# Stacking the real and imaginary state parts on 128 partitions for the mixer's output products

## The chip, the cores and the metric

The kernel runs on one core of one Trainium2 chip, as one program. The metric is device time in microseconds (us) of one execution. The five engines have their own in-order instruction streams: TensorE (PE in the profile, with its weight loads as PEld), VectorE (DVE), ScalarE (ACT), GpSimd (POOL) and SyncE (SP), which here only issues DMA transfers.

## The reference

One denoising step of a two-layer network with 1024 features, on 128 context tokens and 1024 latent tokens. Each layer has a token mixer and a SwiGLU channel mixer, each followed by a residual and a LayerNorm, with shifts, scales and gates computed from a condition vector (`ada_mod`). The mixer of layer 0 is a bidirectional S5 state space of 64 groups of 16 features with 64 complex states each:

```
bu   = einsum('blgh,gph->blgp', u, bb)            # complex, two directions
s    = linear recurrence of (ab, bu) over l        # forward, and backward
y    = u * d_skip
for d in 0, 1:
    y += einsum('blgp,ghp->blgh', s_re, c_re[d]) - einsum('blgp,ghp->blgh', s_im, c_im[d])
y    = gelu(y);  v = y @ glu_w + glu_b;  out = val * sigmoid(gate)
```

Layer 1 mixes by window means. Outputs are both token streams and the context's final states.

## The kernel before

All arithmetic is fp32. Most of the span is the two layers' weight products on the 1024 latents, which split each operand into two fp32r parts and use three products (L776 to L778). The change is in the state-space mixer of layer 0, which comes before them.

The sequence is cut into chunks of 8 tokens: 128 chunks for the latents (NCL), 16 for the context (NCC). Two groups form a pair, whose states fill 128 partitions: group x of the pair on partitions 64x to 64x+63. A state tile `Z[d]` of direction d is [128, slots, 64], where the last axis is (re or im, 32 group pairs), so the 128 chunk values of one pair and one part lie 64 floats apart. The recurrence over chunks runs on VectorE (`scan_step`, L438 and L443).

The output of a chunk is a sum of products on TensorE: one of the chunk's own inputs `u` with an in-chunk kernel, and one per direction and part of the states with an output table. Tables are built by `ssm_tables` for 8 groups (kt = 0 to 7), sent to DRAM (L509, L544), and fetched again by `load_mo` as one 1.5 MB tile `mo` (L548), once per kt for the context (`ssm_y_ctx`) and once for the latents (`ssm_y`). Because a group's re and im parts lie on the same 64 partitions, each state product has a height of 64: for the latents L611 issues 8 of them per group pair (2 directions, 2 parts, 2 groups), with the table as the stationary operand and `Z` as the moving one. In the context (L566) `Z` is stationary and the table moves. Results of the latents go through a gelu (L616) and to DRAM (`yd`); they are read back as `yr` (L1095), split into xm and xn (L760, L761), and feed the layer's glu product.

Around this, other work fills TensorE: the context's glu and channel mixing (`ffn`, L780; one 512 KB load `raw` feeds 8 products; a later part takes 256 KB loads `rc`), and the modulation `ada` (L148; one 512 KB load `adaw` feeds 4 products). `x_sample` comes in as `xr` (L381) and is transposed (`px`, L386). A timeline scheduler of the framework orders each engine's instructions when the kernel is built, from its own model of costs; buffer counts of the pools (`raw` 3, `adaw` 2, `mo` 3, `yr` 2) bound how far loads run ahead. All weight loads are issued by SP, in order. The result row of the last ada bank (`arow`, `ar`) lies where the pool of `yr` is opened, so the loads of `yr` start only after it. A fp32 product is two matmul records in the profile.

Of the kernel before, what the change touches and what calls it, by code (L numbers as in the profile page):

```python
# [41 lines left out]
class Kernel:  # L42
# [3 lines left out]
    # ---------------------------------------------------------------- helpers  # L46
# [20 lines left out]
    def cmul(self, eng, pool, o_re, o_im, a, b, shape, tag, nb_im=None, p=None):  # L67
        """o = a * b for complex pairs; with nb_im = -b_im the imaginary part comes out negated."""
        (a_re, a_im), (b_re, b_im) = a, b
        given = p  # L70
        for k in range(2):
            if given is None:
                p = pool.tile(shape, F32, tag=tag + "1", name=tag + "1")
            q = pool.tile(shape, F32, tag=tag + "2", name=tag + "2")
            if k == 0:
                eng.tensor_tensor(p, a_re, b_re, op=OP.mult)
                eng.tensor_tensor(q, a_im, b_im, op=OP.mult)
                eng.tensor_tensor(o_re, p, q, op=OP.subtract)
            else:
                eng.tensor_tensor(p, a_re, b_im if nb_im is None else nb_im, op=OP.mult)  # L80
                eng.tensor_tensor(q, a_im, b_re, op=OP.mult)
                eng.tensor_tensor(o_im, p, q, op=OP.add if nb_im is None else OP.subtract)

    # ------------------------------------------------------------- constants
    def consts(self):
        nc, I = self.nc, self.I
        cp = self.cp
        self.ones = cp.tile([128, 128], F32, name="ones")
        nc.vector.memset(self.ones, 1.0 / D)
        self.eps = cp.tile([128, 1], F32, name="eps")  # L90
        nc.vector.memset(self.eps, LN_EPS / (ALPHA * ALPHA))

        r0 = cp.tile([16, 128], F32, name="r0")
        nc.sync.dma_start(r0[0:8, :], I["c"].rearrange("o (k p) -> (o k) p", p=128))
        nc.sync.dma_start(r0[8:16, :], I["c_ctx"].rearrange("(k p) -> k p", p=128))
        p0 = self.psum("pv0")
        nc.tensor.transpose(p0[:, 0:16], r0, self.ident[:16, :16])
        self.cond = cp.tile([128, 8, 32], F32, name="cond")
        nc.vector.memset(self.cond, 0.0)
        nc.scalar.activation(self.cond[:, :, 0:2].rearrange("p k i -> p i k"),  # L100
                             p0[:, 0:16].rearrange("p (i k) -> p i k", i=2), AF.Silu)
        # mod[l]: [128, vec, cond, kt]; vec = sh1, sc1, g1, sh2, sc2, g2
        self.mod = [cp.tile([128, 6, 2, 8], F32, name=f"mod{l}") for l in range(2)]
# [26 lines left out]
    # --------------------------------------------------------- conditioning  # L130
    def ada_steps(self, l, b, pool=None):
        """Columns 2048*b.. of layer l's modulation, for both conditions, in small steps."""
# [45 lines left out]
    # ------------------------------------------------------------------ SSM  # L178
    def ssm_params(self, pool, tmp, ad):
# [31 lines left out]
        self.h0 = self.sk.tile([128, 2, 2, 32], F32, name="h0")   # dir, re/im, gpair  # L211
# [19 lines left out]
        # powers of the discretized diagonal: [128, re/im, exponent 0..8, (dir, gpair)]  # L231
# [12 lines left out]
        # input coefficient  # L244
# [15 lines left out]
        # scan multipliers per direction: [128, dir, (Rr|Rr|-?), ...]  # L260
        rm = self.sk.tile([128, 2, 2, 2, 32], F32, name="rm")      # dir, term, re/im, gpair
# [7 lines left out]
        # B and C with the states on the partitions: [128, re/im, (dir, gpair), 16]  # L269
# [28 lines left out]
    def ssm_modvec(self, pool, tmp, arow):  # L298
        """(1 + sc1) and sh1 per (token in chunk, channel) partition: [128, cond, (sh, sc), g]."""
# [20 lines left out]
    def ssm_u(self, tmp, kt):  # L320
        """u[(s,h), g, chunk]: the modulated mixer input; also the context's residual."""
# [23 lines left out]
    def ssm_u_ctx(self, tmp):  # L345
# [3 lines left out]
        # partitions are (feature tile, chunk)  # L349
# [25 lines left out]
    def load_x(self):  # L375
        """Feature-major residual of the latents."""
# [13 lines left out]
    def ssm_in(self, tmp, d, kt, tp, nb):  # L390
        """Chunk inputs V of direction d's state recurrence for 8 groups, written into the state slots."""
# [41 lines left out]
    def scan_step(self, *steps):  # L433
        """State slots: dst += A^8 src, for each (direction, src, dst); the steps are independent."""
# [37 lines left out]
    def ssm_dskip(self, pool, tmp):  # L472
        """D on the partitions (group of 8, h'): [128, kt]; selector of h == h'; zeroed B blocks."""
# [12 lines left out]
        # block-diagonal B of group pairs: [128 = (group of 2, state), dir, re/im, pair, (group of 2, h')]  # L486
# [4 lines left out]
    def ssm_tables(self, tmp, kt, si):  # L491
        """Output tables and in-chunk kernels of 8 groups, to DRAM in the layout of the output products."""
# [3 lines left out]
        for d in range(2):  # L496
# [12 lines left out]
            nc.sync.dma_start(mo[:, 1024 + 1024 * d:2048 + 1024 * d], tab.rearrange("p r g h j -> p (r g h j)"))  # L509
# [36 lines left out]
    def load_mo(self, tmp, kt):  # L546
        mo = tmp.tile([128, 3072], F32, tag="mo", name="mo", bufs=3)
        self.nc.sync.dma_start(mo, self.mo[kt])  # L548
        return (mo[:, 0:1024].rearrange("p (g m) -> p g m", g=8),
                mo[:, 1024:3072].rearrange("p (d r g m) -> p d r g m", d=2, r=2, g=4))  # L550

    def ssm_y_ctx(self, tmp, kt):
        """Mixer output (after gelu) of the context for 8 groups, feature-major."""
        nc = self.nc
        m, ot = self.load_mo(tmp, kt)
        pss = [self.psum(f"pyc{x}") for x in range(2)]
        for t in range(5):
            for x in range(2):
                for gp in range(4):
# [4 lines left out]
                    else:  # L564
                        d, r = (t - 1) // 2, (t - 1) % 2
                        nc.tensor.matmul(  # L566
                            o, self.Z[d][64 * x:64 * x + 64, NCL + d:NCL + d + NCC, 32 * r + 4 * kt + gp],
                            ot[64 * x:64 * x + 64, d, r, gp, :], start=False, stop=(t == 4))
# [14 lines left out]
        # the last ones stay on chip: partitions (group pair, chunk); a group's features go to its own columns,  # L583
        # the rest of them stay zero
# [12 lines left out]
    def ssm_y(self, tmp, kt):  # L597
        """Mixer output (after gelu) of the latents for 8 groups, to DRAM feature-major."""
        nc = self.nc
        m, ot = self.load_mo(tmp, kt)  # L600
        y = tmp.tile([128, 8, NCL], F32, tag="yl", name="yl", bufs=2)
        py = [self.psum(f"py{x}") for x in range(2)]
        for gp in range(4):
# [4 lines left out]
            for d in range(2):  # L608
                for r in range(2):
                    for x in range(2):  # L610
                        nc.tensor.matmul(  # L611
                            o[x], ot[64 * x:64 * x + 64, d, r, gp, :],
                            self.Z[d][64 * x:64 * x + 64, d:d + NCL, 32 * r + 4 * kt + gp],
                            start=False, stop=(d == 1 and r == 1))
# [77 lines left out]
    def ctx0a(self):  # L692
        """The context's mixer output projection of layer 0."""
# [5 lines left out]
    def ctx0b(self):  # L699
        """The context's channel mixing of layer 0, in steps."""  # L700
# [5 lines left out]
    def ctx1a(self, tmp):  # L706
        """The context's pool mixer."""
# [8 lines left out]
    def ctx1b(self):  # L716
        """The context's channel mixing of layer 1, in steps."""
# [6 lines left out]
    # -------------------------------------------------------- derived vectors  # L724
    def vecs(self, l, b):
        """Per-feature vectors [128, cond, kt] of the residual gates and of LayerNorm + modulation,
        from the b-th pair of the layer's modulation vectors."""
# [22 lines left out]
    # ----------------------------------------------------------------- GEMMs  # L750
    def split(self, pool, src, shape, tag, bufs):
        """src = H + L exactly, both exact in float32r."""
# [10 lines left out]
    def weight(self, b, src, shape):  # L763
        """A block of weights [128, n, m]: raw for the native path, (H, L) for the split one."""
# [21 lines left out]
    def pair(self, b, w, x, name):  # L786
        """Two GEMM tiles that are combined elementwise; w yields their weights."""
# [71 lines left out]
    # ------------------------------------------------------------- LayerNorm  # L859
# [6 lines left out]
    def ln_stats(self, b):  # L866
        """b.x to zero mean and unit variance over the features, in place."""
# [33 lines left out]
    def ln_apply(self, b, l, s, xm=None):  # L901
        """The affine part, in place; with xm, also the modulated input of the channel mixer."""
# [19 lines left out]
    # ------------------------------------------------------------ pool mixer  # L922
    def box(self, pool, src, n_out, k, tag, axis, out=None):
        """Window sums along a zero-padded axis (length n_out + k): src[.., i : i + k]."""
# [18 lines left out]
    def pool_cols(self, tmp, q, gis=range(4)):  # L943
        """Window sums along the grid's rows of its rows 4q .. 4q + 3, summed up over the rows: row r of P holds
        the sum of the rows 0 .. r."""
# [19 lines left out]
    def pool_z(self, tmp, b, i, gi):  # L965
        """(window mean - input) of 8 rows of the grid for one window, split for the product."""
# [75 lines left out]
    # ---------------------------------------------------------------- output  # L1042
    def store(self, b, out, t0):
        """Feature-major [128, 8, tokens] back to rows of tokens."""
# [12 lines left out]
    # ----------------------------------------------------------------- build  # L1057
# [124 lines left out]
class Rows:  # L1182
    """Weights [128, n, m] in tiles of four rows."""
# [39 lines left out]
```

## Time and profile before

| what | us |
|---|---|
| median of 3 runs | 2500.75 (2499.89 to 2501.96) |
| span of the profiled execution, first to last instruction | 2493.0 |
| what lies around it: median less span | 7.75 |
| PE busy in the span | 2296.9 (92%) |
| context's outputs on PE (L566) | 220.9 to 279.1 |
| latents' outputs on PE (L611), the main run | 388.7 to 484.5 |
| loads and first glu products that follow | 484.5 to 581.8 |

The profiled execution has no time of its own beside its span; the 7.75 us are the difference to the median and are taken as fixed. PE's 92% is an average: the first 580 us hold most of its idle time, where weights are loaded, and from about 580 us on it is nearly always busy. What a change in the mixer is worth is read from the stretch between 300 and 640 us.

### The profile page before, as it was taken

Reading aid. Unit: us, or ns where it says so; the run is one execution under the profiler, and the core shown is the slowest. Engines: PE = TensorE matmul, PEld = TensorE weight load, DVE = VectorE, ACT = ScalarE, POOL = GpSimd, SP = SyncE. Lnnn points to the kernel's source line nnn. Section 1 sums busy time; section 2 is a strip of 40 time slices with the busy share of each in tenths; the row PEclk is TensorE's granted clock in tenths of the full one; section 3 lists DMA queues with packets and bytes.
Section 4 is the critical chain, followed back from the end, with each engine's and each line's share of the span. In section 5 each row is a group of like instructions: output and inputs, shape, how many; then the busy total and the mean of one; then the engine's idle time right before and its main releaser. Section 6 shows DMA issues by size and latency. Waiting matters only on the chain.

```text
span 2493.0 us, 33897 instructions
## 1 busy us (share of the span) xinstructions
PE 2296.9 (92%) x13533; PEld 1880.8 (75%) x13533; DVE 1252.8 (50%) x2429; ACT 895.0 (36%) x1321; POOL 191.2 (8%) x190
## 2 busy tenths in 40 slices
PE   4685779979999999999999999889999999999997
PEld 2453557668888788888888888777788888888996
DVE  7579771024444632455422585778422455422476
ACT  3673211134423422433422353325322443322464
POOL 4760000000001000100000010002000100000000
PEclk8897889999999999999999999999999999999998
DMA  7767888796454333223333224874333223333352
GB/s 219 218 203 286 278 262 262 219 313 178 142 156 129 101 93 100 95 98 96 94 98 97 99 96 137 236 204 142 94 96 97 95 93 95 92 97 96 136 202 103
DMA packets 465246, 370.63 MB, mean 149 GB/s; under 512 B 19792, under 2 KB 414816, under 8 KB 462784
## 3 DMA queue, kind: packets, MB, share of 16 engines
q1 hardware_dynamic: 445296, 349.29, 45.5%
q10 hardware_dynamic: 18448, 14.58, 1.8%
q0 software_dynamic: 1344, 4.59, 0.5%
q8 instruction: 106, 1.74, 0.3%
q14 instruction: 52, 0.43, 0.1%
HBM read 345.36 MB, written 22.94 MB: 148 GB/s over the span
## 4 chain that ended last, share of the span: by engine, by line
PE 79%; DMA 13%; ACT 3%; DVE 2%; SPq 1%; issue 1%; POOL 1%; ACTq 0%; DVEq 0%; POOLq 0%
PE ffn L778 13%; PE ffn L776 13%; PE ffn L777 13%; PE dn L777 6%; PE dn L776 6%; PE dn L778 6%; PE ffn L780 4%; DMA adaw<-ada_w 3%; PE py L611 3%; PE dn L780 2%; DMA raw<-ffn_w_up 2%; PE glu L777 2%; PE glu L778 2%; PE glu L776 2%; DMA raw<-ffn_w_gate 2%; PE ada L148 1%
## 5 line engine op out<-in xcount | busy, mean ns | idle before, releaser
L760 ACT ACTIVATE wh<-raw 128x1024 fp32r<-128x1024 f32 (+1 forms) x326 | 341.6, 1049 | 944.0 <-PE ffn L777 619.6
L761 DVE TENSOR_TENSOR wl<-raw,wh 128x1024 fp32r<-128x1024 f32 (+1 forms) x326 | 394.6, 1211 | 482.9 <-ACT wh L760 475.5
L777 PE MATMUL dn<-hkl,wh 128*128 128x512 f32 (+1 forms) x880 | 304.3, 348 | 0.3 <-DVE hkl L761 0.3
L778 PE MATMUL dn<-hkh,wl 128*128 128x512 f32 (+1 forms) x880 | 302.9, 347 | 0.0
L776 PE MATMUL ffn<-xp,wh 128*128 128x512 f32 x704 | 280.3, 398 | 2.3 <-ACT wh L760 2.3
L778 PE MATMUL ffn<-xp,wl 128*128 128x512 f32 x704 | 280.5, 398 | 0.5 <-DVE wl L761 0.5
L777 PE MATMUL ffn<-xp,wh 128*128 128x512 f32 x704 | 278.1, 395 | 0.0
L776 PE MATMUL ffn<-xm,wh 128*128 128x512 f32 x704 | 273.3, 390 | 2.8 <-ACT wh L760 2.1
L778 PE MATMUL ffn<-xm,wl 128*128 128x512 f32 x704 | 275.7, 392 | 0.0
L777 PE MATMUL ffn<-xm,wh 128*128 128x512 f32 x704 | 274.9, 390 | 0.2 <-DVE xm L761 0.2
L776 PE MATMUL dn<-hkh,wh 128*128 128x512 f32 (+1 forms) x880 | 259.4, 347 | 0.8 <-ACT hkh L760 0.8
L821 DVE TENSOR_TENSOR h<-ffn,sg 128x512 f32<-128x512 f32 x88 | 60.5, 688 | 254.0 <-PE ffn L778 253.3
L777 PEld LDWEIGHTS dn<-hkl,wh 128*128 128x128 f32 x880 | 166.6, 189 | 21.1 <-DVE hkl L761 0.5
L778 PEld LDWEIGHTS dn<-hkh,wl 128*128 128x128 f32 x880 | 166.5, 189 | 20.5
L776 PEld LDWEIGHTS dn<-hkh,wh 128*128 128x128 f32 x880 | 163.3, 189 | 21.8 <-ACT hkh L760 1.3
L780 PE MATMUL ffn<-xmc,raw 128*128 128x128 f32 x1184 | 150.1, 284 | 23.4 <-DMA raw<-ffn_w_gate 10.6
L780 PEld LDWEIGHTS ffn<-xmc,raw 128*128 128x128 f32 x1184 | 142.3, 197 | 37.7 <-DMA raw<-ffn_w_up 13.9
L776 PEld LDWEIGHTS ffn<-xp,wh 128*128 128x128 f32 x704 | 132.7, 189 | 34.1 <-ACT wh L760 2.5
L777 PEld LDWEIGHTS ffn<-xp,wh 128*128 128x128 f32 x704 | 132.9, 189 | 33.8 <-issue 0.7
L778 PEld LDWEIGHTS ffn<-xp,wl 128*128 128x128 f32 x704 | 132.9, 189 | 33.8 <-DVE wl L761 1.0
L776 PEld LDWEIGHTS ffn<-xm,wh 128*128 128x128 f32 x704 | 132.5, 188 | 32.2 <-ACT wh L760 3.0
L777 PEld LDWEIGHTS ffn<-xm,wh 128*128 128x128 f32 x704 | 132.5, 188 | 28.4 <-DVE xm L761 0.9
(305 smaller groups left out, 3209.5 us busy)
## 6 DMA issues: line engine op xcount, KB each, us to landing
raw<-ffn_w_down SPq DMA_DIRECT2D x126, 512.0 KB
raw<-ffn_w_gate SPq DMA_DIRECT2D x125, 512.0 KB
raw<-ffn_w_up SPq DMA_DIRECT2D x125, 512.0 KB
adaw<-ada_w SPq DMA_DIRECT2D x96, 512.0 KB
raw<-ssm_glu_w SPq DMA_DIRECT2D x48, 512.0 KB
mo<-mo SPq DMA_DIRECT2D x16, 1536.0 KB
rc<-ffn_w_down SPq DMA_DIRECT2D x40, 256.0 KB
mo<-otab SPq DMA_DIRECT2D x16, 512.0 KB
```

The costliest lines, as they stand in the source:

```text
L148: nc.tensor.matmul(ps[32 * cg:32 * cg + 32, 256 * hf:256 * hf + 256], self.cond[:, k, :], w[:, cg * 256:(cg + 1) * 256], start=(k == 0), s ...
L611: nc.tensor.matmul(o[x], ot[64 * x:64 * x + 64, d, r, gp, :], self.Z[d][64 * x:64 * x + 64, d:d + NCL, 32 * r + 4 * kt + gp], start=False, ...
L760: nc.scalar.activation(h, src, AF.Copy)
L761: nc.vector.tensor_tensor(l, src, h.bitcast(F32), op=OP.subtract)
L776: nc.tensor.matmul(ps, wh, xh, start=start, stop=False)
L777: nc.tensor.matmul(ps, wh, xl, start=False, stop=False)
L778: nc.tensor.matmul(ps, wl, xh, start=False, stop=stop)
L780: nc.tensor.matmul(ps, w[0], x[0], start=start, stop=stop)
L821: nc.vector.tensor_tensor(h[:, f, :], pu, sg, op=OP.mult)
```

## The change

`ssm_tables` writes the tables so that a group's re rows lie on partitions 0 to 63 of `mo` and its im rows on 64 to 127; one DMA per direction becomes two. A new `stack` rearranges `Z` in place to fit: three copies of 64 partitions per direction and kt, on ScalarE for direction 0 and on VectorE for direction 1. After it the first half of the last axis holds group 0 of each pair (re over im), the second group 1. One product of height 128 per group and direction then stands for two of height 64. `mo` has 2 buffers and no longer 3. The removal of comments is left out below.

```diff
@@ ssm_tables
-            nc.sync.dma_start(mo[:, 1024 + 1024 * d:2048 + 1024 * d], tab.rearrange("p r g h j -> p (r g h j)"))
+            for x in range(2):
+                c0 = 1024 + 1024 * d + 512 * x
+                nc.sync.dma_start(mo[:, c0:c0 + 512].rearrange("(r p) f -> p r f", r=2),
+                                  tab[64 * x:64 * x + 64].rearrange("p r g h j -> p r (g h j)"))
@@ load_mo
-        mo = tmp.tile([128, 3072], F32, tag="mo", name="mo", bufs=3)
+        mo = tmp.tile([128, 3072], F32, tag="mo", name="mo", bufs=2)
-                mo[:, 1024:3072].rearrange("p (d r g m) -> p d r g m", d=2, r=2, g=4))
+                mo[:, 1024:3072].rearrange("p (d x g m) -> p d x g m", d=2, x=2, g=4))
+    def stack(self, tmp, kt, c0, n, tag):
+        nc = self.nc
+        for d in range(2):
+            z = self.Z[d][:, c0 + d:c0 + d + n, :].rearrange("p c (r g) -> p r g c", r=2)[:, :, 4 * kt:4 * kt + 4]
+            t = tmp.tile([64, 4, n], F32, tag=tag, name=tag, bufs=2)
+            if d == 0:
+                cp = lambda o, i: nc.scalar.activation(o, i, AF.Copy)
+            else:
+                cp = lambda o, i: nc.vector.tensor_copy(o, i)
+            cp(t, z[64:128, 0])
+            cp(z[64:128, 0], z[0:64, 1])
+            cp(z[0:64, 1], t)
@@ ssm_y_ctx
+        self.stack(tmp, kt, NCL, NCC, "swc")
-        for t in range(5):
+        for t in range(3):
...
-                        d, r = (t - 1) // 2, (t - 1) % 2
-                        nc.tensor.matmul(
-                            o, self.Z[d][64 * x:64 * x + 64, NCL + d:NCL + d + NCC, 32 * r + 4 * kt + gp],
-                            ot[64 * x:64 * x + 64, d, r, gp, :], start=False, stop=(t == 4))
+                        d = t - 1
+                        nc.tensor.matmul(o, self.Z[d][:, NCL + d:NCL + d + NCC, 32 * x + 4 * kt + gp],
+                                         ot[:, d, x, gp, :], start=False, stop=(t == 2))
@@ ssm_y
+        self.stack(tmp, kt, 0, NCL, "swl")
-            for d in range(2):
-                for r in range(2):
-                    for x in range(2):
-                        nc.tensor.matmul(
-                            o[x], ot[64 * x:64 * x + 64, d, r, gp, :],
-                            self.Z[d][64 * x:64 * x + 64, d:d + NCL, 32 * r + 4 * kt + gp],
-                            start=False, stop=(d == 1 and r == 1))
+            for x in range(2):
+                for d in range(2):
+                    nc.tensor.matmul(o[x], ot[:, d, x, gp, :], self.Z[d][:, d:d + NCL, 32 * x + 4 * kt + gp],
+                                     start=False, stop=(d == 1))
```

The scheduler arranges the changed program anew. In the changed kernel lines after the new code are 17 higher: L780 is L797, L611 is L630, L607 is L627.

The first place is TensorE in the latents' outputs. `py` is the result of a group, `Z_648` and `Z_1796` (`Z_1812` in the changed kernel) are the two directions' states. A part of one group pair before:

```order
L607 MATMUL py_4668<-u,mo 128x128
L607 MATMUL py_4669<-u,mo 128x128
L611 MATMUL py_4668<-Z_648,mo 128x128
L148 MATMUL ada_4215<-adaw_4234,cond 32x256 x4
L611 MATMUL py_4669<-Z_648,mo 128x128
L611 MATMUL py_4668<-Z_648,mo 128x128
L611 MATMUL py_4669<-Z_648,mo 128x128
```

A whole group pair in the changed kernel:

```order
L627 MATMUL py_4572<-u,mo 128x128
L627 MATMUL py_4573<-u,mo 128x128
L630 MATMUL py_4572<-Z_648,mo 128x128
L630 MATMUL py_4572<-Z_1812,mo 128x128
L630 MATMUL py_4573<-Z_648,mo 128x128
L630 MATMUL py_4573<-Z_1812,mo 128x128
```

Before, a pair has 4 state products of each direction; in the changed kernel it has 2 of each.

The second place is TensorE from the last latents' output on. Before:

```order
L611 MATMUL py_4669<-Z_1796,mo 128x128
L780 MATMUL ffn<-xmc,raw 128x128 x8
L148 MATMUL ada_4215<-adaw_4240,cond 32x256 x4
L780 MATMUL ffn<-xmc,raw 128x128 x4
L148 MATMUL ada_4215<-adaw_4246,cond 32x256 x4
L780 MATMUL ffn<-xmc,raw 128x128 x20
L148 MATMUL ada_4215<-adaw_4252,cond 32x256 x4
L148 MATMUL ada_4215<-adaw_4258,cond 32x256 x4
L780 MATMUL ffn<-xmc,raw 128x128 x24
```

In the changed kernel:

```order
L630 MATMUL py_4573<-Z_1812,mo 128x128
L797 MATMUL ffn<-xmc,raw 128x128 x4
L148 MATMUL ada_4057<-adaw_4148,cond 32x256 x4
L797 MATMUL ffn<-xmc,raw 128x128 x28
L386 MATMUL px<-ident,xr_5035 128x128 x3
L160 MATMUL adat_4161<-ident,ar_4156 128x32
L386 MATMUL px<-ident,xr_5035 128x128 x5
L148 MATMUL ada_4167<-adaw_4168,cond 32x256 x4
L386 MATMUL px<-ident,xr_5049 128x128 x8
L148 MATMUL ada_4167<-adaw_4174,cond 32x256 x4
L386 MATMUL px<-ident,xr_5063 128x128 x8
```

Counted over the whole lists: before, 112 `ffn` products stand ahead of the main run of outputs, none in it and 128 behind it, with 18 groups of `ada` in it and 12 behind; in the changed kernel 144 stand ahead, 64 within and 32 behind, with 12 groups of `ada` within and 17 behind, 16 of which are the whole last bank.

The third place is SP's queue of loads at the end of the stage. Before:

```order
L769 DMA raw<-ffn_w_gate 128x8x128
L769 DMA raw<-ffn_w_up 128x8x128
L146 DMA adaw_4300<-ada_w 128x1024
L146 DMA adaw_4306<-ada_w 128x1024
L381 DMA xr_5147<-x_sample 128x1024
L381 DMA xr_5161<-x_sample 128x1024
L381 DMA xr_5175<-x_sample 128x1024
```

In the changed kernel:

```order
L786 DMA raw<-ffn_w_gate 128x8x128
L146 DMA adaw_4168<-ada_w 128x1024
L786 DMA raw<-ffn_w_up 128x8x128
L381 DMA xr_5035<-x_sample 128x1024
L381 DMA xr_5049<-x_sample 128x1024
L146 DMA adaw_4174<-ada_w 128x1024
L381 DMA xr_5063<-x_sample 128x1024
L381 DMA xr_5077<-x_sample 128x1024
L146 DMA adaw_4180<-ada_w 128x1024
```

Before, all `adaw` loads stand ahead of the 8 loads of `xr` and the glu weights; in the changed kernel 15 of the last 16 `adaw` loads stand behind or among the 8 `xr` loads and the first 6 glu loads, the last 7 of them in a row.

## Rows read from the trace of the kernel before

**Rows 1.** The chain that ended last: its shares of the whole span by line.

```profile
PE ffn L778 13%; PE ffn L776 13%; PE ffn L777 13%; PE dn L777 6%; PE dn L776 6%; PE dn L778 6%; PE ffn L780 4%; DMA adaw<-ada_w 3%; PE py L611 3%; PE dn L780 2%; DMA raw<-ffn_w_up 2%; PE glu L777 2%; PE glu L778 2%; PE glu L776 2%; DMA raw<-ffn_w_gate 2%; PE ada L148 1%
```

**Rows 2.** Stretches: length, busy us of each engine, granted clock, DMA share, GB/s.

```profile
core 0: us, PE busy (x) PEld busy (x) DVE busy (x) ACT busy (x) POOL busy (x), PEclk, DMA share, GB/s
300.00:388.00 88.00, 68.90 (x575) 53.90 (x568) 67.48 (x368) 13.50 (x29) 5.72 (x8) 0.88 0.88 266
388.70:484.50 95.80, 95.80 (x757) 68.48 (x756) 0.83 (x4) 10.12 (x18) 0.00 (x0) 1.00 0.70 231
484.50:530.30 45.80, 38.06 (x353) 31.30 (x352) 2.33 (x8) 4.23 (x11) 0.00 (x0) 1.00 1.01 308
530.30:581.80 51.50, 41.18 (x249) 34.17 (x250) 22.90 (x28) 30.70 (x40) 4.31 (x8) 0.97 0.94 286
```

**Rows 3.** Lines of PE from 388.7 to 484.5: records, busy us, mean ns.

```profile
L611 PE MATMUL py<-Z,mo 64*128 64x128 f32 x492 | 69.2, 404 | 0.0
L607 PE MATMUL py<-u,mo 128*128 128x128 f32 x118 | 21.7, 303 | 0.0
L148 PE MATMUL ada<-adaw,cond 128*32 128x256 f32 x144 | 11.3, 390 | 0.0
```

**Rows 4.** Timeline of PE, 389 to 393: start, duration, group of records.

```profile
389.77 0.71 PE L607 MATMUL py<-u,mo 128*128 128x128 f32 x4
390.41 2.00 PE L611 MATMUL py<-Z,mo 64*128 64x128 f32 x16
392.34 0.71 PE L607 MATMUL py<-u,mo 128*128 128x128 f32 x4
```

**Rows 5.** Timeline of PE at 390.4 and up to 390.89: two records, then four.

```profile
390.41 0.47 PE L611 MATMUL py<-Z,mo 64*128 64x128 f32 x2
...
390.41 0.69 PE L611 MATMUL py<-Z,mo 64*128 64x128 f32 x4
```

**Rows 6.** Timeline of PE after 484 us.

```profile
484.45 2.05 PE L780 MATMUL ffn<-xmc,raw 128*128 128x128 f32 x16
```

**Rows 7.** Records of L611: ns shortest, median, longest; first and last start.

```profile
L611 PE MATMUL py<-Z,mo x512: 390/392/464, 371.8 to 484.1; 64*128 64x128 f32 x171
```

**Rows 8.** Records of L607, the same columns.

```profile
L607 PE MATMUL py<-u,mo x128: 275/275/377, 283.6 to 481.1; 128*128 128x128 f32 x128
```

**Rows 9.** Timeline of PE in the context's outputs, one kt.

```profile
233.97 0.63 PE L563 MATMUL pyc<-mo,u 128*16 128x128 f32 x16
234.53 1.21 PE L566 MATMUL pyc<-mo,Z 64*16 64x128 f32 x64
```

**Rows 10.** Timeline of all engines, 380 to 390: the scan's end, the outputs' start.

```profile
382.87 0.48 DVE L443 TENSOR_TENSOR Z<-stt,Z 128x64 f32<-128x64 f32 x2
...
388.72 1.12 PE L611 MATMUL py<-Z,mo 64*128 64x128 f32 x8
```

**Rows 11.** Lines of ACT from 366 to 490: the gelu and its wait.

```profile
L616 ACT ACTIVATE yl<-py 128x512 f32<-128x512 f32 x16 | 8.7, 594 | 82.7 <-PE py L611 82.7
```

**Rows 12.** The copy of L458 on VectorE.

```profile
L458 DVE COPY Z<-h x1: 186/186/186, 219.8 to 219.8; 128x64 f32<-128x64 f32 x1
```

**Rows 13.** DMA from 388.7 to 484.5: bytes, and loads issued.

```profile
DMA packets 11867, 22.11 MB, mean 231 GB/s; under 512 B 532, under 2 KB 8801, under 8 KB 11221
...
adaw<-ada_w SPq DMA_DIRECT2D x18, 512.0 KB
mo<-mo SPq DMA_DIRECT2D x5, 1536.0 KB
```

**Rows 14.** The tile yr: first and last load, split operations, landing time.

```profile
L1095 POOL DMA_DIRECT2D yr<-yd x8: 530/530/587, 536.1 to 572.6; - x8
L760 ACT ACTIVATE xm<-yr x8: 1120/1135/1185, 543.6 to 576.7; 128x512 fp32r<-128x512 f32 x8
L761 DVE TENSOR_TENSOR xm<-yr,xm x8: 1100/1166/1237, 544.8 to 577.9; 128x512 fp32r<-128x512 f32 x8
...
DMA to landing us min/median/max: 4.0/6.8/8.7
```

## The prediction

> **What bounds the kernel now.** I read the chain of waits first: most of the span is the latents' weight products, which the change leaves alone, and the mixer's state products (L611) hold 3% of it [rows 1]. Then I cut the time around them into stretches [rows 2]. From 300 to 388 us PE is busy for 68.9 of 88 us and the DMA engines for 0.88 of the time: loads bind. From 388.7 to 484.5 us PE has no gap, the clock is 1.00, and DMA moves 231 GB/s where the next stretch moves 308: PE binds. From 484.5 to 581.8 us DMA is at 1.01 and 0.94 and PE waits: loads bind again. So only the middle stretch is open to cheaper products, and what is gained there meets a full DMA queue behind it.
>
> **Products of the latents.** A group pair takes from 389.77 to 392.34, that is 2.57 us, with 4 records of u and 16 of Z [rows 4]. From two records to four the run grows from 0.47 to 0.69 us [rows 5]: the half-height records run as pairs (both groups of a pair at once), a pair per 0.22 us. A full-height record of contiguous columns costs (2.05 - 0.275) / 15 = 0.118 us [rows 6, 8]. So a half-height pair is nearly twice a contiguous record. Its duration agrees: 392 ns against 275, longer by 117, one more streaming time [rows 7, 8].
>
> Two things differ between these rows: the pair shares the array, and Z moves with a stride of 64 floats while the others are contiguous. The context's outputs part them. There the tables move, contiguous, and Z is stationary: 64 half-height records take 1.21 us [rows 9], or 0.019 us each. Eight run at once (two row halves, four column blocks), in 8 waves of (1.21 - 0.27) / 7 = 0.13 us. If the row halves took turns, 16 waves would need at least 16 x 0.118 = 1.9 us. Sharing rows therefore costs nothing there, and I put the doubling down to the stride. The changed kernel still moves Z with that stride, now for all 128 partitions, so I price a full-height Z record at 0.22 us, no less than the pair it replaces. The Trainium skill, "SBUF — State Buffer", section "Specifications (TRN2)", gives the memory lines of 16 bytes and says that full bandwidth needs at least two accesses to a line and that each step to a new line is penalised. By that rule every column of Z pays, at whatever height, and the sum below stays as it is; without it the full-height product would cost 0.118 and the sum would be the first rival's. The rows on Z agree with it (392 against 275 ns), but no row shows a strided product of full height.
>
> What remains of a pair's 2.57 us is 2.57 - 4 x 0.118 - 8 x 0.22 = 0.34 us, the two changes between full and half height. These go, since u and Z now have one height. A group pair then costs 4 x 0.118 + 8 x 0.22 = 2.23 us. The stretch holds 492 of 512 Z records [rows 3], some 31 pairs: a saving of 31 x 0.34 = 10.5 us. At 0.118 a pair would cost 1.42 us and the saving would be 36 us.
>
> **What else stands in the stretch.** Before, 18 groups of ada cost 11.3 us [rows 3]; with 31 x 2.57 = 79.7 that leaves 95.8 - 91.0 = 4.8 us for entering and leaving 18 groups, 0.13 a time. In the changed order 12 groups (7.5 us and 24 x 0.13 = 3.1) and 64 ffn products stand there, which are 128 records x 0.118 = 15.1 us. The sum is 31 x 2.23 + 7.5 + 3.1 + 15.1 = 94.8 us. So the products' saving is used up by the ffn work that moved in, and the stretch stays near 95.8.
>
> **Its start.** Ahead of it the order has 32 more ffn products (4 raw loads) and one more ada load, 5 x 0.524 = 2.6 MB, and one 1.57 MB mo load less, since mo has two buffers. That is 1.05 MB more in a stretch bound by loads at 266 GB/s [rows 2], 3.9 us; some of it runs ahead and I take 3. The end of the outputs then moves by 3 - 1 = +2 us.
>
> **Behind the outputs.** Before, it takes 45.8 us from the last output to the last ada product and 51.5 more to 581.8 us, where the glu is in full run [rows 2]. The loads of yr wait for the last ada row: they start at 536.1, 5.8 us after that product [rows 14]. In the changed order the end of the last bank stands behind 4 raw, 17 adaw, 8 xr and 6 glu loads, 35 x 0.524 = 18.3 MB, of which up to 2.6 MB (3 raw and 2 adaw buffers) can have landed. At 308 GB/s that is 51 to 59 us; I take 57, since the last 7 adaw go through two buffers with nothing else to fill the queue. Then yr: before, 45.7 us from its first issue to 581.8, at 286 GB/s shared with xr, glu and rc loads. After, xr and six glu loads are done. A yr costs 4.0 us to land at least, and its buffer is held for one ACT and two DVE operations more, 1.14 + 2 x 1.17 [rows 14]; with two buffers that is 3.7 us a yr, 30 for eight. Between 30 and 45.7 I take 37. Sum: 57 + 5.8 + 37 = 100 against 97.3, +2.5 us. Beyond, 11 of the context's rc products, which ran inside the wait, are left for the PE-bound part: 22 x 0.118 = +2.6 us.
>
> **The copies of stack.** In the latents 24 run on each of ACT and DVE, 64 partitions by 512 elements. No row shows this form. The nearest are the gelu of 512 elements at 594 ns and a VectorE copy of 64 elements at 186 ns [rows 11, 12]; I take 0.6. A kt needs three in a row, 1.8 us, while PE works some 11.8 us on a kt, DVE has 0.8 us of work in the stretch and ACT waits 82.7 us for PE [rows 2, 11]: covered. Only the first is open, and 383.35, the scan's end, lies 5.4 us ahead of the first main product [rows 10]. If the cover fails for every kt, it is 8 x 1.8 = 14 us. The context's 48 copies are of 64 elements, 0.2 us; 24 on DVE are 4.8 us in the scan's stretch, and the 5.4 us cover them.
>
> **Products of the context.** 64 half-height records in 8 waves become 32 of full height, four at once, also 8 waves: no gain. The 16 added table DMAs are 2 per direction with the same bytes, in a stretch where I see no reason for a loss above 1 us; nothing is set down.
>
> **Sum.** +2 + 2.5 + 2.6 = +7.1 us on the profiled span of 2493.0, so 2500; with the 7.75 us around it, 2508 against the median of 2500.75. The chips' runs of this kernel agree within 0.1%; a change below 0.2%, 5 us, is none that can be told.
>
> **Rivals.**
> Half rate belongs to the pairing (faster). Then Z records cost 0.118 and the outputs could take 31 x 1.42 + 25.7 = 70 us. But they must load 12 adaw, 8 raw and 6 mo and store 7 yl, 23.6 MB (before, 22.11 [rows 13]), 77 us at 308 GB/s. The end moves by 3 + 77 - 95.8 = -16 us, the sum is -11: 2490. For it: no row has a full-height strided product. Against: the context's row halves. Chance 0.22.
>
> The loads are spread better (no change). If the 18.3 MB land in 51 us and yr in 33, what follows is 90 instead of 100, and the sum is -3: 2498. For it: the queue has xr and glu early, and PE work is inside the stretch. Against: the two-buffer ring at the end of the bank. Chance 0.22.
>
> The copies or the two mo buffers hold PE up (slower). If each kt waits for its stack or its mo, behind an adaw on SP, for 1 to 2 us, that adds 8 to 16 us to my sum: 2516 to 2524. It decides as soon as a kt's three copies start later than 1.8 us before its first product, on ACT behind an sg that waits for ffn loads. Chance 0.14.
>
> **Chances and range.** My forecast has 0.42, its own range is 2502 to 2514, a quarter of it within the 5 us. Faster by over 0.2%: the first rival and a third of the second, 0.30. Within: the rest of the second and part of the forecast, 0.26. Slower: 0.44. The range reaches from the first rival's 2490, a little below, to the middle of the third: 2487 to 2519.
>
> **What would show it.** Right: a timeline of a group pair with 12 records in about 2.2 us and Z records of 392 ns; no gap of PE behind stack copies; yr loads starting 60 us or more behind the last output. Wrong: Z records of 275 ns, 0.118 us apart (first rival); the outputs ending before 475; yr issued sooner than 55 us behind them (second); ACT or DVE copies as releaser of L630 (third).

## The result, and the profile after

The changed kernel takes 2514.6 us (median of 5 runs, 2508.63 to 2522.07) against 2499.89 for the kernel before (5 runs, 2494.85 to 2501.96): a ratio of 1.0064, 95% interval 1.0048 to 1.008, that is 12 to 20 us slower. It was forecast slower, at 2508, in a range of 2487 to 2519. The profiled executions differ by 15.0 us (spans of 2508.0 and 2493.0).

One number ahead of the sum was misread. In each run of the changed kernel the time is 1.8 us above the span (2509.8 and 2508.0); the 7.75 us of the table before were therefore 1.8 us around the span and 6 us of spread between runs. Both profiled executions lie at the low end of their kernel's runs, so their traces can be set against each other.

The outputs come first. In the timeline of TensorE in the changed kernel (start, duration, group of records), a group pair now reads:

```profile
481.93 0.62 PE L627 MATMUL py<-u,mo 128*128 128x128 f32 x4
482.39 1.91 PE L630 MATMUL py<-Z,mo 128*128 128x128 f32 x8
484.12 0.62 PE L627 MATMUL py<-u,mo 128*128 128x128 f32 x4
```

From 481.93 to 484.12 it is 2.19 us, where [rows 4] had 2.57 with twice as many Z records. The eight Z records of the pair follow each other at 0.22 us (482.39 to 484.12). The tile Z in the changed kernel (shortest, median and longest ns, first and last start) gives the records and the new copies:

```profile
L630 PE MATMUL py<-Z,mo x256: 376/395/467, 378.1 to 486.1; 128*128 128x128 f32 x128
...
L564 ACT ACTIVATE swl<-Z x8: 1053/1094/1507, 374.9 to 415.7; 64x512 f32<-64x512 f32 x8
...
L566 DVE COPY swl<-Z x8: 727/798/890, 391.8 to 415.4; 64x512 f32<-64x512 f32 x8
```

A record takes 395 ns, like the 392 ns of the half-height one in [rows 7], and not the 275 ns of [rows 8]. A full-height record takes a half-height pair's time, so halving the count left the products' streaming where it was. The lines of TensorE from 394.5 to 486.5, which answer to [rows 3], show what fills the stretch instead (records, busy us, mean ns):

```profile
L630 PE MATMUL py<-Z,mo 128*128 128x128 f32 x252 | 61.5, 396 | 0.0
L627 PE MATMUL py<-u,mo 128*128 128x128 f32 x120 | 19.4, 280 | 0.0
L797 PE MATMUL ffn<-xmc,raw 128*128 128x128 f32 x132 | 16.5, 277 | 0.0
L148 PE MATMUL ada<-adaw,cond 128*32 128x256 f32 x96 | 7.7, 391 | 0.0
```

The outputs end at 486.5 us, 2 later than before. The loss comes behind them. The stretches of the changed kernel (length, busy us of PE, PEld, DVE, ACT and POOL, granted clock, DMA share, GB/s), first all from 300 us to the 72nd glu product, at 594.5, where the glu is in full run, and then its parts:

```profile
300.00:594.50 294.50, 232.94 (x1649) 188.82 (x1650) 118.11 (x466) 98.03 (x128) 9.92 (x16) 0.88 0.82 255
300.00:388.00 88.00, 67.93 (x569) 54.18 (x570) 70.35 (x393) 16.81 (x33) 5.62 (x8) 0.90 0.88 271
388.00:486.50 98.50, 98.50 (x662) 87.38 (x655) 23.72 (x41) 47.48 (x51) 0.00 (x0) 1.00 0.86 271
486.50:551.00 64.50, 33.91 (x265) 19.38 (x264) 4.70 (x8) 15.08 (x25) 0.00 (x0) 0.73 0.82 261
551.00:594.50 43.50, 32.60 (x162) 27.88 (x163) 19.34 (x24) 18.66 (x20) 4.30 (x8) 0.78 0.58 176
```

In the kernel before, the same point of the glu comes at 581.8:

```profile
300.00:581.80 281.80, 244.65 (x1936) 188.45 (x1929) 93.54 (x408) 58.55 (x97) 10.03 (x16) 0.96 0.85 265
```

Length times rate is 74.7 MB before and 75.1 MB after. About the same amount has to be moved from 300 us to that point, and the changed kernel moves it at 255 GB/s, not 265. The 12.7 us between 581.8 and 594.5 are nearly all of the loss. Where [rows 2] moved 308 and 286 GB/s behind the outputs, it is 261 and then 176, and TensorE, waiting, falls to a granted clock of 0.73. Its timeline shows the last ada groups and the wait for the ada row:

```profile
547.02 1.08 PE L148 MATMUL ada<-adaw,cond 128*32 128x256 f32 x8 [1.66 <-DMA adaw<-ada_w]
549.77 1.08 PE L148 MATMUL ada<-adaw,cond 128*32 128x256 f32 x8 [1.66 <-DMA adaw<-ada_w]
555.03 0.28 PE L160 MATMUL adat<-ident,ar 32*128 32x32 f32 x1 [4.18 <-DMA ar<-arow]
```

The last two groups start 2.75 us apart, and a group is 1.08 us long where it is 0.64 at full clock. SP's timeline has the seven loads in a row:

```profile
527.55 18.20 SPq L146 DMA_DIRECT2D adaw<-ada_w  x7
```

Half a MB each 2.6 us is some 200 GB/s. Each load waits for a buffer of the ring: a group on TensorE, and then the load that takes over its buffer, issued 0.07 us after the group's end:

```profile
539.03 1.08 PE L148 MATMUL ada<-adaw,cond 128*32 128x256 f32 x8 [1.68 <-DMA adaw<-ada_w]
...
540.18 0.33 SPq L146 DMA_DIRECT2D adaw<-ada_w  x1
```

The loads of yr then start 20 us later than in [rows 14] (tile yr of the changed kernel):

```profile
L1112 POOL DMA_DIRECT2D yr<-yd x8: 527/530/588, 555.8 to 586.3; - x8
...
DMA to landing us min/median/max: 3.9/4.5/7.8
```

They land sooner, 4.5 us and not 6.8, with only 14 half-size `rc` loads beside them: most of the other loads are done by then, and the queue moves 176 GB/s while yr passes through its two buffers.

### The profile page after: what moved, and what is told of

Read it like the earlier page. It is cut to its first block, busy times and chain, and to the rows that moved or that the text cites. A ratio compares the mean times of both kernels' runs of the same rounds, so it can differ in the third digit from the quotient of the medians.

```text
span 2508.0 us, 33004 instructions
## 1 busy us (share of the span) xinstructions
PE 2287.3 (91%) x13021; PEld 1885.2 (75%) x13021; DVE 1278.6 (51%) x2477; ACT 946.4 (38%) x1379; POOL 187.2 (7%) x190
## 4 chain that ended last, share of the span: by engine, by line
PE 75%; DMA 8%; DVE 3%; issue 1%; ACT 1%; POOL 0%; ACTq 0%; SPq 0%; DVEq 0%; POOLq 0%
PE ffn L795 13%; PE ffn L794 13%; PE ffn L793 13%; PE dn L794 6%; PE dn L793 6%; PE dn L795 6%; PE ffn L797 4%; PE dn L797 2%; PE py L630 2%; PE glu L794 2%; PE glu L795 2%; PE glu L793 2%; DMA raw<-ffn_w_up 2%; DMA adaw<-ada_w 2%; DMA raw<-ffn_w_gate 1%
## 5 line engine op out<-in xcount | busy, mean ns | idle before, releaser
L778 DVE TENSOR_TENSOR wl<-raw,wh 128x1024 fp32r<-128x1024 f32 (+1 forms) x326 | 394.5, 1210 | 502.4 <-ACT wh L777 474.1
L797 PE MATMUL ffn<-xmc,raw 128*128 128x128 f32 x1184 | 152.4, 286 | 22.8 <-DMA raw<-ffn_w_gate 11.2
L797 PEld LDWEIGHTS ffn<-xmc,raw 128*128 128x128 f32 x1184 | 144.6, 199 | 36.5 <-DMA raw<-ffn_w_up 14.0
L793 PEld LDWEIGHTS ffn<-xm,wh 128*128 128x128 f32 x704 | 132.1, 188 | 32.3 <-ACT wh L777 3.0
L795 PEld LDWEIGHTS ffn<-xm,wl 128*128 128x128 f32 x704 | 132.2, 188 | 28.0 <-issue 0.7
```

The source lines that it names most:

```text
L778: nc.vector.tensor_tensor(l, src, h.bitcast(F32), op=OP.subtract)
L793: nc.tensor.matmul(ps, wh, xh, start=start, stop=False)
L795: nc.tensor.matmul(ps, wl, xh, start=False, stop=stop)
L797: nc.tensor.matmul(ps, w[0], x[0], start=start, stop=stop)
```

## The experiments

Each time is a median; each ratio is to runs of the kernel before on the same chip. The labels are explained below the table. "Glu" is the start of the 72nd glu product in the kernel's trace, MB and GB/s count from 300 us to it.

| kernel | us | ratio (95%) | glu | MB | GB/s |
|---|---|---|---|---|---|
| before | 2499.89 | 1 | 581.8 | 74.7 | 265 |
| changed | 2514.6 | 1.0064 (1.0048 to 1.008) | 594.5 | 75.1 | 255 |
| tie_xr | 2516.77 | 1.007 (1.0058 to 1.0082) | 596.8 | 75.4 | 254 |
| ad3 | 2480.98 | 0.9933 (0.9916 to 0.995) | 568.0 | 76.9 | 287 |
| contig_z | 2495.09 | 0.9979 (0.9967 to 0.9992) | 575.5 | 76.0 | 276 |
| no_latent_copies | 2514.7 | 1.0071 (1.0058 to 1.0085) | 594.5 | 74.8 | 254 |
| contig_z_ad3 | 2469.49 | 0.9887 (0.9865 to 0.9909) | 546.6 | 76.4 | 310 |
| before_mo2 | 2513.14 | 1.0055 (1.0034 to 1.0075) | 596.6 | 77.4 | 261 |
| before_mo2_ad3 | 2506.06 | 1.0043 (1.0026 to 1.006) | 583.6 | 75.7 | 267 |
| stack_psum_mo2 | 2521.94 | 1.0086 (1.0066 to 1.0106) | 601.2 | 77.1 | 256 |
| stack_psum_mo3 | 2517.7 | 1.0067 (1.0049 to 1.0085) | 600.2 | 76.0 | 253 |
| stack_psum_ad4 | 2488.78 | 0.9952 (0.9935 to 0.9969) | 568.0 | 75.6 | 282 |

**Order of the loads alone (tie_xr).**

```diff
@@ load_x
+            if q == 0:
+                nc.vector.tensor_copy(xp[:, 0:2], self.mod[1][:, 4, :, 0])
             nc.sync.dma_start(xp, xs[128 * q:128 * q + 128, :])
```

> The changed kernel with one tiny copy added, which makes the first load of x_sample wait for the last ada bank; products, copies and buffers stay. The last ada loads then stand ahead of all xr and glu loads, as before the change. Theory (the loss of 15 us lies in the order of loads behind the outputs): the outputs still end at about 486 us, the last ada product comes at about P + 47 instead of P + 64, yr starts at about P + 53, and the time goes back to within 4 us of the kernel before. Rival (the loss is in copies and products): yr moves, but the time stays 10 us or more above the kernel before.

The ada products did end sooner, at 538 us for 551, and yr started at 543.2 for 555.8, though 5 and 4 us later behind the outputs than the theory had them. The time stayed. In its stretches, the one from the outputs to the last ada product:

```profile
486.50:538.50 52.00, 25.93 (x199) 11.63 (x198) 1.13 (x5) 2.84 (x5) 0.00 (x0) 0.61 0.60 182
```

With little but the 16 ada loads in it the queue moves 182 GB/s, and what had been loaded beside them comes later. My theory as put (the order) falls; the rival on copies is not shown by it either. What both orders share is the ring of two buffers with some 16 loads behind the outputs.

**A third ada buffer (ad3).**

```diff
@@ ada_steps
-            return q.tile([128, n], F32, tag="ad", name=name, bufs=4 if pool else 2)
+            return q.tile([128, n], F32, tag="ad", name=name, bufs=4 if pool else 3)
```

> The changed kernel with three buffers for the ada loads instead of two; the scheduler then keeps most of the last bank ahead of xr. Theory (order of loads, and the two-buffer ring that leaves DMA at 230 GB/s behind the outputs): the stretch from the outputs to the glu moves 280 GB/s or more, and the time is 5 to 15 us under the changed kernel, at or a little under the kernel before. Rival (copies and products): within 4 us of the changed kernel.

The theory's direction holds, with more than it said: 19 us under the kernel before, 34 under the changed one. (The profiled execution is the slowest of its six, 2489.3 us. Its glu is 13.8 us ahead of that of the kernel before, its end 5.5: 8 us are lost again behind 1497 us, in the second layer.) Its stretches, from 300 us to the glu and from 486.5 to the last ada product:

```profile
300.00:568.00 268.00, 233.87 (x1705) 196.83 (x1704) 119.51 (x464) 99.87 (x131) 10.21 (x16) 0.94 0.92 287
486.50:517.30 30.80, 27.28 (x249) 20.81 (x247) 1.46 (x5) 4.95 (x10) 0.00 (x0) 1.00 0.95 303
```

Its timeline of TensorE shows why: a group of ada and 16 records of ffn take turns, so two kinds of buffers are being filled at once, and the clock stays at 1.00.

```profile
505.22 0.64 PE L148 MATMUL ada<-adaw,cond 128*32 128x256 f32 x8
506.26 2.05 PE L797 MATMUL ffn<-xmc,raw 128*128 128x128 f32 x16 [0.40 <-DMA raw<-ffn_w_up]
508.24 0.64 PE L148 MATMUL ada<-adaw,cond 128*32 128x256 f32 x8
```

The ring's size and the scheduler's new order came together here; tie_xr shows that an order with the ada loads first does not do it with two buffers.

**A contiguous moving operand (contig_z).** The latents' stack writes a tile of its own, [128, group of the pair, pair, chunk], instead of Z.

```diff
+    def stack_c(self, tmp, kt, n):
...
+            t = tmp.tile([128, 2, 4, n], F32, tag=f"sz{d}", name=f"sz{d}", bufs=1)
+            for x in range(2):
+                for r in range(2):
+                    o, i = t[64 * r:64 * r + 64, x], z[64 * x:64 * x + 64, r]
+                    if d == 0:
+                        nc.scalar.activation(o, i, AF.Copy)
+                    else:
+                        nc.vector.tensor_copy(o, i)
...
@@ ssm_y
-        self.stack(tmp, kt, 0, NCL, "swl")
+        sz = self.stack_c(tmp, kt, NCL)
...
-                    nc.tensor.matmul(o[x], ot[:, d, x, gp, :], self.Z[d][:, d:d + NCL, 32 * x + 4 * kt + gp],
+                    nc.tensor.matmul(o[x], ot[:, d, x, gp, :], sz[d][:, x, gp, :],
```

> The changed kernel with the latents' stacked states copied into a tile of their own with the 128 chunks side by side, so that the moving operand is contiguous; 8 copies a direction pair of 64 partitions instead of 6, one buffer each. Theory (the stride sets the rate): a state record takes 275 ns and records follow 0.118 us apart, half of the 395 ns and 0.22 us before; a group pair takes 1.4 us where copies don't hold it up; the whole gains little or loses, since the copies of the next kt wait for the products of the last and the order of loads behind is the same. Rival (a full-height product with this table costs 0.22 us whatever the layout): 395 ns and 0.22 us stay.

Its timeline of TensorE, and the record of the tile:

```profile
468.18 0.61 PE L644 MATMUL py<-u,mo 128*128 128x128 f32 x4
468.62 1.06 PE L647 MATMUL py<-sz,mo 128*128 128x128 f32 x8
469.51 0.61 PE L644 MATMUL py<-u,mo 128*128 128x128 f32 x4
```

```profile
L647 PE MATMUL py<-sz,mo x256: 275/275/377, 380.3 to 470.7; 128*128 128x128 f32 x128
```

A pair takes 1.33 us for 2.19 and the record 275 ns for 395. Height, table and count are those of the changed kernel; only the distance of the columns differs. The stride set the rate. The outputs end at 471 us, 15 earlier, and the glu comes 19 us earlier: more than the theory allowed, which had put the gain down as lost behind the outputs. During the outputs the queue moves 349 GB/s, where the changed kernel moved 271:

```profile
388.00:471.00 83.00, 79.69 (x722) 71.36 (x721) 30.41 (x56) 56.58 (x61) 0.00 (x0) 1.00 1.02 349
```

The time is just under the kernel before.

**Without the latents' copies (no_latent_copies).** The call of `stack` in `ssm_y` is removed: this kernel leaves out the rearranging of the latents' states, so its latents' outputs are not the network's.

> The changed kernel without the copies of stack for the latents, so that the latents' state products take unstacked states: this part of the computation is left out. Theory (copies are hidden, all but the first): the outputs end 0 to 4 us sooner, and the time is within 4 us of the changed kernel. Rival (copies hold TensorE up, or delay the outputs' start by some 6 us): 6 us or more faster than the changed kernel.

2514.7 against 2514.6: the 24 copies on each engine are hidden, though one takes 1.09 us on ScalarE and 0.80 on VectorE. The rival falls. The outputs do not start sooner either; the main run of them begins at 395.1, that of the changed kernel at 394.5:

```profile
395.13 1.04 PE L629 MATMUL py<-Z,mo 128*128 128x128 f32 x4
```

**Both causes taken away (contig_z_ad3).** The edits of contig_z and ad3, and one buffer for the context's copy tile.

> The changed kernel with the contiguous stacked tile for the latents and three ada buffers (and one buffer for the small copy tile of the context). Theory (two separate causes: the stride sets the products' rate, the two-buffer ada ring starves DMA behind the outputs): the gains add in part, since both end in the same DMA-bound stretch: the outputs end by about 475 us, the glu is in full run 16 us or more ahead of the kernel before, and the time is 2472 to 2482 us. Rival (the gains are one and the same): as with three ada buffers alone, 2481 us or more.

The gains add in large part: 2469.5 us, 45 under the changed kernel, where contig_z alone was 20 and ad3 alone 34 under it. That is 29 us under the kernel before (1.1%), a little below the range that the theory gave. From 300 us to its glu:

```profile
300.00:546.60 246.60, 210.07 (x1704) 173.99 (x1705) 124.77 (x474) 106.69 (x139) 10.21 (x16) 0.93 0.97 310
```

DMA is busy for 0.97 of the stretch. This version beats both kernels.

**The kernel before with two mo buffers (before_mo2)**, and with three ada buffers as well **(before_mo2_ad3).**

```diff
@@ load_mo, both
-        mo = tmp.tile([128, 3072], F32, tag="mo", name="mo", bufs=3)
+        mo = tmp.tile([128, 3072], F32, tag="mo", name="mo", bufs=2)
@@ ada_steps, the second only
-            return q.tile([128, n], F32, tag="ad", name=name, bufs=4 if pool else 2)
+            return q.tile([128, n], F32, tag="ad", name=name, bufs=4 if pool else 3)
```

> The kernel before with two mo buffers, all else as it was, half-height products too. The scheduler then leaves 10 ada groups behind the outputs and puts most ffn loads behind them. Theory (the loss comes from 17 ada groups on two buffers behind the outputs, without loads beside them): this kernel has raw loads between its ada loads there, DMA stays near 300 GB/s, and the time is within 6 us of the kernel before. Rival (a third mo buffer is itself worth the loss): 10 us or more slower than the kernel before.

> The kernel before (half-height products) with two mo buffers and three ada buffers; the scheduler puts all ada groups inside the outputs and all but 48 ffn products behind them. Theory (three ada buffers are worth time by keeping DMA busy, whatever the height of the products): faster than the kernel before, 2478 to 2494 us, the rest to the changed kernel with three buffers being the 10 us of mode changes. Rival (the full-height products are needed for the gain): within 5 us of the kernel before or slower.

Both theories fall, and the rivals' times come. With two mo buffers the half-height kernel loses 15 us, as much as the change does. Its stretch to the glu:

```profile
300.00:596.60 296.60, 254.06 (x1966) 200.77 (x1965) 94.71 (x394) 59.85 (x101) 10.21 (x16) 0.92 0.85 261
```

But it loses them in another place, ahead of the outputs: at 236 GB/s from 300 to 388 us (266 in [rows 2]), and with 69.1 MB moved by 300 us against 71.5, while 280 GB/s flow from 484 us to the glu. With three ada buffers it moves 296 GB/s in that first stretch, and 246 GB/s from 388 to 484 us. The stretch of before_mo2, and then the two of before_mo2_ad3:

```profile
300.00:388.00 88.00, 67.53 (x522) 55.01 (x521) 64.27 (x344) 12.80 (x27) 5.91 (x8) 0.80 0.79 236
300.00:388.00 88.00, 68.12 (x603) 49.69 (x603) 65.02 (x348) 13.59 (x27) 6.11 (x8) 0.92 0.95 296
388.00:484.00 96.00, 95.50 (x771) 68.79 (x768) 1.71 (x10) 11.44 (x20) 1.13 (x2) 1.00 0.73 246
```

The glu of before_mo2_ad3 is 1.8 us behind that of the kernel before, its 288th glu product 4.5 us, and the end of its span 9.4 us. In this kernel the third ada buffer is worth 7 us (2513.14 to 2506.06), with overlapping intervals, where it was worth 34 in the changed kernel. No run has the kernel before with three ada buffers and all three of its mo buffers.

**The third mo buffer given back (stack_psum_mo2, stack_psum_mo3, stack_psum_ad4).** The copy tile in PSUM frees the space. The first is the control.

```diff
@@ stack, all three
-            t = tmp.tile([64, 4, n], F32, tag=tag, name=tag, bufs=2)
+            t = self.psum(tag)[0:64, 0:4 * n].rearrange("p (g c) -> p g c", g=4)
@@ load_mo, stack_psum_mo3 only: bufs=2 -> bufs=3
@@ ada_steps, stack_psum_ad4 only: bufs=4 if pool else 2 -> bufs=4 if pool else 4
```

> The changed kernel with the small copy tile of stack in PSUM instead of SBUF, mo still with two buffers: the control of the next run. The order behind the outputs has 16 ada groups on two buffers, as in the changed kernel. Both theories: within 6 us of the changed kernel, 2506 to 2520 us.

> As the last, with the third mo buffer back (the space comes from the copy tile that went to PSUM). The order keeps 21 ada groups on two buffers and all xr loads behind the outputs, with 97 ffn products among them. Theory A (two mo buffers cost the 14 us, as in the kernel before with two buffers): back within 5 us of the kernel before, or under it by the mode changes' 10 us. Theory B (ada groups left behind the outputs on two buffers cost it, whatever mo has): 10 us or more above the kernel before, as 21 are left instead of 17, each some 2.5 us apart.

> The changed kernel with the copy tile in PSUM, two mo buffers and four ada buffers; the order has no ada group behind the outputs and 128 ffn products there. Theory B (what counts is the ada bank behind the outputs): yr starts before the outputs end, and the time is 2475 to 2490 us. Theory A (two mo buffers cost it): slower than the kernel before by 5 us or more.

The control is 7 us above the changed kernel, a little past its range; its outputs end at 502 us, 16 later than in the changed kernel. Of its 22 us over the kernel before, the third mo buffer gives back some 4; four ada buffers give back 33, although yr starts 7 us after the outputs' end and not ahead of it, as theory B had it. Of the two theories as put, B holds and A falls in this kernel: the time goes with the ada loads that are left behind the outputs. What a mo buffer is worth by itself is not isolated, since the order of stack_psum_mo3 leaves 21 ada groups there and the control's leaves 16. Stretch to the glu of stack_psum_mo3, where the outputs had ended by 477 us, and of stack_psum_ad4:

```profile
300.00:600.20 300.20, 238.29 (x1711) 192.56 (x1706) 127.05 (x495) 87.02 (x123) 10.07 (x16) 0.90 0.80 253
300.00:568.00 268.00, 230.67 (x1698) 195.32 (x1699) 127.06 (x472) 99.53 (x132) 9.93 (x16) 0.93 0.90 282
```

## Why the prediction was right, and which terms were off

- **The number.** The forecast was +7.1 us, and 14.7 were measured. Its own range, 2502 to 2514, ends just short of 2514.6; the stated range reaches on to 2519 only for the third rival, that copies or mo buffers hold TensorE up, and TensorE has no gap from 388 to 486.5 us. So it is partly luck that the time lies in the range.
- **Rate of the full-height product.** Put at 0.22 us with a pair at 2.23; measured 2.19. That the stride is the reason, argued from the context's outputs, is shown by contig_z. The rule of the Trainium skill that was weighed there ("SBUF — State Buffer", section "Specifications (TRN2)", a penalty for each step to a new line of 16 bytes) agrees: 395 ns with a stride of 256 bytes, 275 without. The first rival falls.
- **The outputs' start and end.** The start was put at +3, measured some +6 (394.5 for 388.7). The 32 added ffn products stand ahead of the start as forecast; the copies are not the reason for the rest of the +6, as no_latent_copies shows. The sum of the stretch, 94.8 us, came out at 92. The end was put at +2 and is at +2 (486.5 for 484.5): two small errors cancelled.
- **Behind the outputs, the mis-sized term.** From the last output to the glu in full run, 100 us against 97.3 were forecast, +2.5; measured 108 (486.5 to 594.5), +10.7. Its first part was "57" at 308 GB/s and took 64.5 at 261: the two-buffer ring was named, but only 6 us were added to the 51 that full speed allows, and the fall of the clock, which lengthens a group in the ring from 0.64 to 1.08 us, was not in it. Eleven of the 17 groups are that long; as they alternate between two buffers, an estimate is that this makes 5.5 x 0.44 = 2.4 us of the 7.5. The rest is not split further. The last step, from the ada row to the glu, was 43 and took 43.5. The other 8 us of the 15 lie in that one term.
- **The rc products left over.** +2.6 put down; the distance of the two kernels grows by 2.5 us between the 72nd and the 288th glu product (12.7 to 15.2), and 70 records of rc products stand between the two, where the kernel before has 48.
- **Products of the context.** No gain was forecast, and there is none. At the lower clock (granted 0.50 in both) the state products of one kt take 1.97 us before and 1.93 in the changed kernel:

```profile
240.20 1.97 PE L566 MATMUL pyc<-mo,Z 64*16 64x128 f32 x64
...
242.10 1.93 PE L586 MATMUL pyc<-mo,Z 128*16 128x128 f32 x32
```

- **Copies.** Put at 0.6 us, measured 0.80 and 1.09, and hidden as said. The third rival (copies or mo hold TensorE up) falls for the copies.
- **No change** (the loads better spread) was wrong about this order, though ad3 shows that the mechanism exists.

What stays open: which edit brings the order about. Every edit here, a buffer count too, made the scheduler arrange loads and fill work anew, and no run has the changed products in the order before. Shown is that 75 to 77 MB are moved from 300 us to the glu in each of these kernels, at 253 to 310 GB/s, and 144.7 to 146.6 MB from the start of the span to it. With the bytes so nearly fixed, a late glu is a low mean rate by arithmetic; what held the rate down has to be read from the waits, kernel by kernel. That a two-buffer ring of ada loads with little beside it runs at 182 GB/s is shown too. Not explained is why before_mo2_ad3 loses another 5 us in the second layer and ad3 loses 8 there: there is one trace of each kernel, and the runs of one kernel spread by 2 to 16 us.

## What to carry to other kernels

In products like these, count a matmul by its streamed columns and the distance between them, not by its height: two half-height products that ran at once took the time of one of full height. In a group pair stacking took 2.57 us to 2.19, and adjacent columns then took it to 1.33. When a stage sits between load-bound stretches, sum the bytes up to the next bound point and ask for the mean rate there: in stack_psum_mo3 the outputs ended 9 us sooner than in the changed kernel and the glu started 6 us later. And where a scheduler orders the program, read the load queue again after any edit, buffer counts first.

## What had not been expected

TensorE's clock fell with its idle time behind the outputs: granted 0.73 in the changed kernel and 0.61 in tie_xr, where it had been busy for 34 of 64.5 and 26 of 52 us, against 1.00 in ad3 (27 of 31). At the lower of its two levels (1.2 and 2.4 GHz) the ada group took 1.08 us and not 0.64, and the next load of the ring was issued only after it, so a shortage of loads lengthened itself. And copies of 512 elements on 64 partitions from columns 256 bytes apart took 1.09 us on ScalarE and 0.80 on VectorE, where the gelu of 512 elements from PSUM takes 0.59 [rows 11].
